# One transfer for the first slice of G, a shorter warm-up, one more pair loaded slice by slice, and a new written-out order, in a weight-gradient matmul

## The chip, the cores and the metric

The kernel runs on one core of a Trainium2 chip. The metric is the time of one launch on the device in microseconds (us); smaller is better. The profile names the engines PE (TensorE matmul), PEld (TensorE weight load), DVE (VectorE), ACT (ScalarE), POOL (GpSimd) and SP (SyncE, which here only issues transfers).

## The reference: what is computed

```python
batch, m, k, n = 16, 512, 1024, 768
grad_weight = np.einsum('bmk,bmn->kn', input, grad_output)   # float32 in, float32 out
```

Batch and m are both summed over, so with X as 8192 x 1024 and G as 8192 x 768 the output is X transposed times G, 1024 x 768.

## The kernel before

**Slices and blocks.** The 8192 rows are cut into 64 slices of 128 rows, two slices to a load entry u = 0 to 31 (`LOADS`). A matmul takes 128 columns of an X slice as weights and half of a G row, 384 columns, as the moving operand. The output has four quadrants: A (upper half of K, left half of N), B (upper, right), C (lower, left), D (lower, right), each of four blocks q = 0 to 3 of 128 rows. A token such as `C2` means block 2 of quadrant C.

**Plain entries and pairs.** Entries of kind "s" (u = 0 to 3 and 31, ten slices) are multiplied directly, 16 matmuls a slice. Entries of kind "P" (u = 4 to 30, 27 pairs) are multiplied in the manner of Strassen and Winograd: seven products of sums instead of eight products, so 28 matmuls a pair and not 32. The products are summed in the blocks 1, 5, 6, 7 and in A, B and C. The operand sums are made by DVE in bfloat16, three for X (`x0.u`, `x1.u`, `x2.u`, lines 199, 201, 203) and three for G (`g0.u` to `g2.u`, lines 209, 211, 213). At the end the blocks are joined: the close of a last block adds the block that it shares (line 360, DVE; lines 355 and 356 for a 5 block), and for some blocks a merge `w` does that addition ahead of time on POOL, from SBUF to SBUF (line 395).

**Loads.** Slices 0 and 1 of X and slice 0 of G come as float32 over the queues of ACT and SP (lines 145 to 148) and are rounded to bfloat16 by DVE and ACT (`round_by`, line 217). All else comes over POOL's queue, which rounds on the way: entry u = 1 one slice at a time (lines 175 and 177), entries from `MERGED` = 2 on as one transfer of G and one of X (lines 170 and 171). All the transfers of POOL stand ahead of its merges in its order.

**Order.** Nothing is scheduled by a compiler on PE, DVE, ACT and POOL: the string `PLAN` is the order of work, token by token, and every engine runs its part of it in that order. `C2@5.1` opens block C2 in PSUM bank 5 and multiplies it by one item (slice or pair); `C2.3` goes on for three items. `cC2` closes a block with ACT where it may and `vC2` with DVE (a copy if the sum in SBUF is new or was carried along, else an addition, lines 363, 365, 367). `fC2@5` copies the running sum back into a bank with ACT (line 295), so that the next close is a copy. `z` and `y` lay a partial sum aside and add it later (lines 379 and 388), `r` is a rounding. A bank can be opened or filled again only when its close has read it. Blocks A0 to A3 share the banks 0 to 2 throughout and are closed at the very end. A last close is followed by the store of its block, on SP, and on ACT for a part of the last (line 342).

**Warm-up.** Until the first data are there PE multiplies constants (`WARMUP`, line 153): one bfloat16 matmul of 512 columns, two float32 ones of 512, one bfloat16 one of 512. A float32 one is two instructions in the trace.

**The roundings at the start.** Before the plan's first token DVE rounds G columns 0 to 191, X columns 0 to 127, 128 to 255 and 512 to 767, and ACT rounds G columns 192 to 383, X columns 256 to 511 and 768 to 1023; the right half of G and all of slice 1 follow as tokens `r0` to `r4`.

Of the kernel before, what the change touches and what calls it, by code (L numbers as in the profile page):

```python
# [9 lines left out]
P = 128  # L10
# [5 lines left out]
    "A0.1 A2.1 C0@7.1 A3.1 C2@6.1 cC0 r0 C3@3.1 C1@4.1 cC2 A1.1 vC3 B1@5.1 cC1 B2@7.1 D3@6.1 r1 D0@3.1 r4 r2 "  # L16
    "D1@4.1 cB1 D1.1 A0.1 B2.1 cD1 D0.1 B0@5.1 cD3 A3.1 vD0 A2.1 r3 A1.1 B3@6.1 vB0 cB2 B3.1 D3@4.1 B0@3.1 "
    "D2@7.1 vD3 D2.2 B0.1 vB3 B1@5.1 cD2 B1.1 A3.1 C3@4.1 vB1 C3.1 C2@6.2 vC3 A2.1 B3@7.1 C1@5.3 B3.1 B0.1 "
    "vC1 A1.2 C2.1 vB3 B1@4.1 D1@5.1 zcC2.20 D1.1 vB1 B2@7.2 A0.1 vB0 A0.1 A2.1 vD1 D3@6.2 D0@4.1 vB2 D0.1 "
    "A3.1 C3@5.1 vD0 D2@3.1 C0@7.2 vD3 C0.2 vD2 C0.1 C3.2 B3@6.2 vC3 B1@3.2 A3.1 vC0 D3@5.2 vB1 A1.2 B2@4.1 "  # L20
    "vD3 B2.1 D2@3.1 A0.1 yC2.20 A0.1 A3.1 D0@7.1 vB2 D0.1 A2.2 vD2 B0@5.2 D1@4.1 vD0 D1.3 vB0 C0@7.2 A3.1 "
    "vD1 A3.1 A1.1 vC0 B3.1 D2@5.3 fC1@7 B3.1 D0@4.1 vD2 D0.1 A0.2 vD0 fD3@5 C1.3 vB3 C1.1 A2.2 g0.4 cC1 "
    "C3@4.1 B2@6.1 fC2@3 B2.1 g1.4 D3.2 fB0@7 vB2 C3.1 C2.1 cD3 C2.1 g2.4 C2.1 x0.4 C2.2 A2.1 12@5.1 cC2 C3.1 "
    "x1.4 A1.2 c12 x2.4 11@6.1 C0@3.1 fC1@5 vC3 B0.3 c11 vC0 A3.1 C1.1 A0.1 B3@6.1 cC1 61@3.1 B1@4.1 vB3 cB0 "
    "B1.2 c61 73@5.1 g0.5 71@6.1 10@7.1 vB1 13@3.1 x0.5 13.1 A1.1 12@4.1 c13 10.1 A3.1 v12 71.1 c10 73.1 "
    "50@3.1 x1.5 c71 50.1 11@4.1 g1.5 51@7.1 c50 51.1 v11 60@6.1 c73 60.1 61@3.1 g0.6 c51 A2.1 53@5.1 v61 "
    "53.1 fC0@4 A0.1 63@7.1 c53 g2.5 63.1 52@3.1 g1.6 52.1 70@5.1 g2.6 70.1 c52 C0.1 x0.6 C0.1 A1.1 A3.1 cC0 "
    "72@3.1 x2.5 72.2 x1.6 70.1 73@4.1 A0.1 c70 x2.6 63.1 60.1 v73 A2.1 c63 B0@5.2 g0.7 c72 B2@4.2 c60 B2.1 "
    "vB0 62@7.1 fC1@3 62.1 g1.7 62.1 B3@6.1 vB2 B3.1 c62 C1.2 g2.7 C2@4.1 fC0@7 vB3 C2.2 f13@5 C1.1 x0.7 A2.1 "
    "A0.1 cC1 C0.1 11@6.1 vC2 11.1 f51@3 A1.1 13.1 v11 13.1 51.2 x1.7 c13 A3.1 53@6.1 cC0 x2.7 53.1 52@4.1 "  # L30
    "c51 52.1 v53 71@5.2 f50@7 C3@3.1 g0.8 C3.1 f12@6 C3.1 50.1 g1.8 50.1 12.1 g2.8 12.2 x0.8 A2.1 C3.1 c12 "
    "A1.1 A3.1 vC3 52.1 71.1 50.1 x1.8 zc52.20 73@6.2 v71 fB1@3 A0.1 61@4.2 x2.8 c50 61.1 72@5.1 v73 72.1 "
    "fB2@7 B1.2 v72 f10@6 B1.2 B2.1 v61 B2.1 cB1 63@5.1 g0.9 63.1 f51@4 10.3 fC2@3 x0.9 10.1 A1.1 cB2 A3.1 "
    "A2.1 g1.9 51.1 zc63.5 x1.9 51.1 62@7.1 c10 g2.9 62.2 x2.9 c51 A0.1 C2.1 v62 fB3@5 C2.1 60@6.2 y63.5 60.1 "
    "fB0@7 B3.2 v60 cC2 B3.1 11@4.2 y52.20 cB3 B0.2 f13@3 g0.10 B0.1 53@6.2 cB0 13.1 x0.10 13.2 f70@7 A3.1 "
    "11.1 g1.10 c13 A1.1 53.1 x1.10 70.1 f52@5 70.1 v11 70.2 A0.1 g2.10 fB2@4 52.1 x2.10 52.1 C1@3.1 c70 v53 "
    "C1.2 c52 B2.1 C3@7.1 vC1 C3.1 f72@5 B2.1 C0@6.1 vC3 C0.1 cB2 C0.1 72.1 g0.11 f73@3 B1@7.2 A2.1 c72 x0.11 "
    "A2.1 A1.1 f71@4 73.2 vC0 73.1 f63@5 71.1 g1.11 71.1 c73 71.1 x1.11 A0.1 72@6.1 c71 g2.11 72.1 63.1 x2.11 "
    "63.1 fB0@4 63.1 v72 61@3.2 c63 61.1 g0.12 B0.1 fC2@6 B0.1 60@5.1 v61 60.1 cB0 A3.1 g1.12 C2.2 v60 12@3.2 "
    "cC2 12.1 x0.12 12.1 fC3@4 B1.1 A1.1 A2.1 f53@5 g2.12 A3.1 vB1 C3.1 f51@6 C3.1 53.1 v12 53.1 cC3 50@7.2 "  # L40
    "x1.12 50.1 fC1@4 50.1 g0.13 A0.1 c53 51.2 x2.12 51.1 C1.1 g1.13 B3@5.1 c51 B3.1 v50 B3.1 f13@3 C1.1 "
    "52@6.1 vB3 52.1 cC1 13.2 x0.13 13.1 f62@4 11@5.2 c13 11.1 x1.13 A0.1 62.1 v52 62.1 f70@3 62.2 g2.13 "
    "61@7.2 c62 x2.13 70.2 v61 fC0@6 70.1 B2@4.2 v11 c70 B2.1 C0.2 vB2 f71@3 C0.1 A3.1 f73@7 10@5.1 g0.14 "
    "10.3 B1@4.1 x0.14 A2.2 zcB1.4 71.2 10.1 x1.14 f51@4 71.1 73.1 g1.14 73.1 c71 x2.14 73.1 51.1 g2.14 51.1 "
    "c73 A1.2 v10 c51 A0.1 B3@7.1 g0.15 cC0 B3.1 A3.1 63@3.1 vB3 fB1@6 63.2 B0@5.1 g1.15 f70@4 B0.1 v63 B0.1 "
    "B1.2 g2.15 72@7.2 cB1 vB0 72.1 70.1 C2@3.1 x0.15 f52@5 C2.3 53@6.2 vC2 53.1 70.1 52.1 v53 52.2 72.1 "
    "x1.15 f11@6 C1@3.2 v72 C1.1 c52 A2.1 A0.1 vC1 c70 13@7.2 60@5.1 yB1.4 f10@3 60.2 g0.16 60.1 11.2 x0.16 "
    "11.1 10.2 c11 13.1 v60 A1.2 f62@4 A3.1 x1.16 A3.1 f71@6 A2.1 v13 50@5.3 g1.16 50.1 f12@7 g0.17 62.2 "
    "zc50.18 62.1 12.1 g1.17 12.1 c62 12.1 g2.16 12.1 x2.16 71.1 fB1@4 71.1 g2.17 C3@5.1 c12 C3.1 x2.15 C3.2 "
    "x0.17 C3.1 10.1 A2.1 C0@7.1 c10 vC3 C0.2 c71 C0.1 x1.17 A3.1 A0.1 fB2@6 x2.17 A0.1 B0@3.1 g0.18 B0.2 "  # L50
    "B2.1 vC0 B2.3 vB0 B1.3 g1.18 C2@7.2 cB1 g2.18 73@5.2 cB2 vC2 73.1 C1@3.1 f61@4 C1.1 x0.18 C1.1 A1.1 "
    "zc73.3 51@6.2 vC1 51.2 C2@5.1 x1.18 fB3@3 61.2 vC2 61.3 x2.18 f53@5 63@7.2 g0.19 63.1 c61 63.1 53.2 v63 "
    "f52@4 53.1 B3.2 g1.19 f12@7 B3.1 v51 B3.1 A0.1 c53 52.1 12.1 cB3 12.1 13@5.1 x0.19 f71@6 13.2 12.1 "
    "72@3.1 x1.19 72.2 v13 72.1 71.2 v12 71.1 70@5.2 g0.20 70.1 f60@7 70.1 52.1 v72 52.2 60.1 g1.20 60.1 c52 "
    "x2.19 60.2 c71 A1.1 v70 A1.1 11@3.1 f10@6 g2.19 11.2 x0.20 11.1 fB3@5 10.3 v11 A3.2 c10 A3.1 x1.20 A2.1 "
    "fB1@3 73@4.1 x2.20 73.2 g0.21 B3.1 60.1 62@6.1 v73 62.1 c60 62.2 g2.20 B1.1 C0@4.1 g1.21 C0.1 cB1 y50.18 "
    "C0.1 C2@7.1 cB3 C2.1 g2.21 B1@3.2 v62 fB2@5 A2.3 x0.21 B2.3 vC0 C2.1 71@6.2 zcC2.1 vB1 A0.1 51@4.1 cB2 "
    "51.1 g0.22 51.1 A0.1 f72@5 50@7.1 v71 50.3 g1.22 50.1 C1@3.2 v50 C1.1 72.2 x1.21 C3@7.2 g2.22 c72 C3.1 "
    "v51 C3.2 C1.1 x0.22 A1.3 zcC1.10 12@6.1 f63@5 12.1 x1.22 12.1 53@4.1 f13@3 53.1 v12 53.2 63.1 x2.21 63.2 "
    "x2.22 63.1 B0@6.1 g0.23 B0.1 c63 B0.2 v53 B0.1 A0.1 vC3 A0.1 f70@4 13.3 f52@5 x0.23 13.1 70.2 c13 70.1 "  # L60
    "g1.23 A3.1 fC0@7 x1.23 A3.1 52.1 vB0 52.3 g2.23 61@3.2 g0.24 61.3 70.1 C0.1 v61 C0.1 c70 C0.1 62@6.1 "
    "y73.3 c52 62.2 cC0 x2.23 B3@4.3 g1.24 f71@5 B3.1 v62 A3.2 A0.1 x0.24 A0.1 A2.3 vB3 71.3 x1.24 73@4.2 "
    "yC1.10 c71 73.2 fB2@7 50@6.1 g2.24 50.1 v73 11@5.3 x2.24 B2.1 f60@4 B2.1 v11 B2.1 f62@3 B2.1 60.1 g0.25 "
    "60.1 cB2 60.2 x0.25 A1.3 72@7.1 x1.25 72.2 g1.25 72.1 A3.1 yC2.1 62.1 zc72.15 62.1 60.1 x2.25 A2.1 "
    "B1@5.1 c60 g2.25 B1.2 c62 B1.2 B0@4.1 f10@3 B0.1 vB1 B0.1 53@7.2 g0.26 53.1 10.2 g1.26 10.2 x0.26 10.2 "
    "51@5.2 c10 x1.26 51.2 y72.15 51.1 f52@3 50.1 A3.1 vB0 zc51.21 50.2 A0.1 x2.26 A0.1 fB2@4 63@5.1 g0.27 "
    "63.3 52.1 g1.27 53.1 v50 B2.2 zc53.18 52.1 v63 52.1 cB2 12@6.2 g2.26 12.2 x0.27 12.1 B3@7.2 g2.27 B3.1 "
    "11@4.1 v12 11.3 y53.18 C0@5.3 vB3 C0.1 C2@6.2 g0.28 fC3@7 C2.3 vC0 C2.1 C3.1 g1.28 C3.2 x1.27 C3.2 vC2 "
    "52.1 61@5.1 cC3 61.1 y51.21 61.1 c52 61.1 A2.1 v11 A2.2 13@6.1 x0.28 13.4 x1.28 72@7.2 zc13.12 72.1 "
    "x2.28 61.1 f73@3 70@4.1 v72 70.2 f71@6 70.1 v61 70.1 73.2 g2.28 73.1 x2.27 73.1 C3@5.1 g0.29 71.4 g1.29 "  # L70
    "A2.1 C1@7.1 c71 g2.29 C1.2 c73 x0.29 C1.4 A3.1 g0.30 A3.1 zcC1.4 A3.1 C3.1 f11@3 v70 A1.4 x1.29 f62@4 "
    "12@7.1 g1.30 12.1 A0.1 y13.12 A0.2 11.1 vC3 11.1 10@6.2 x0.30 10.2 11.1 13@5.1 v10 13.1 c11 12.1 62.1 "
    "x1.30 f61@6 62.2 v12 62.1 f72@3 62.1 61.1 v13 f71@7 61.1 A2.1 v62 72.1 f60@5 72.1 71.1 v61 71.1 f51@4 "
    "60.2 g2.30 60.1 f52@6 60.1 v72 60.1 51.2 v60 f70@3 51.1 wC2 51.1 52.1 v71 52.2 A3.1 f63@7 v51 A3.2 70.1 "
    "fC0@5 70.1 63.2 yC1.4 63.1 wD1 63.1 C0.1 v70 C0.1 fC1@4 C0.2 v63 C0.1 A0.2 vC0 fD1@7 A0.1 C1.2 v52 fC2@5 "
    "C1.1 A2.2 f73@3 A1.3 vC1 fB1@6 wD2 D1.2 x2.30 73.2 cD1 x2.29 B1.2 vA3 B1.1 fB2@7 B1.2 v73 fD2@4 B1.2 "
    "C2.1 vA2 C2.1 f53@3 C2.2 vA1 C2.1 53.2 cC2 53.1 vB1 53.1 B2.1 fC3@5 B2.1 v53 B2.1 fD3@2 B2.3 f50@6 C3.1 "
    "vA0 C3.2 wB3 50.1 vB2 50.3 vC3 D2.1 fB0@7 D2.1 D3.1 v50 D3.1 cD2 B0.2 fD0@5 B0.3 fB3@3+4 vD3 B0.2 D0.2 "
    "vB0 B3.4 vD0 B3.2 cB3 "
# [3 lines left out]
WARMUP = [("b", 512), ("f", 512), ("f", 512), ("b", 512)]  # L83
# [369 lines left out]
```

## Time and profile before

| | |
|---|---|
| time of three runs | 161.98 us median (161.97 to 162.1) |
| the profiled execution | 161.87 us, of which its span is 160.1 us |
| PE busy | 154.8 us, 97% of the span |
| DVE busy | 145.1 us, 91% |
| ACT, POOL busy | 99.3 us (62%), 39.1 us (24%) |
| matmuls on data (line 324) | 996 |
| warm-up matmuls | 6 instructions, 0.78 to 5.15 us |
| POOL's transfers from line 170 / 171 | 30 of 384 KB / 30 of 512 KB, as written to SBUF |
| transfers | busy throughout to about 140 us, 209 to 216 GB/s as written |

The time of the profiled execution is 1.77 us more than its span: what lies before the first and after the last instruction. Times in the views are counted from the span's start. PE's instructions overlap: a 384-column matmul shows 326 ns from start to end, while the next one starts 162 ns after it, so a busy share near 100% says only that PE was not idle for long.

### The profile page before, as it was taken

What the parts mean: (1) busy time and instruction counts of PE and PEld (TensorE: products, weight loads), DVE (VectorE), ACT (ScalarE), POOL (GpSimd) and SP (SyncE); (2) the same over time, 40 slices, a digit from 0 to 9 for tenths busy, and PEclk for the clock granted to TensorE, in tenths of its full rate; (3) what the DMA queues carried; (4) which work ended last, traced back from release to release, by engine and by line L of the source; (5) the groups of instructions that cost most, each with busy time, mean ns of one, the idle gap of its engine ahead of it and who ended that gap; (6) DMA issues with size and microseconds to landing.
All of it is one profiled execution on the core that took longest, in us unless ns stands there. A gap on an engine that the chain in (4) does not pass through costs nothing.

```text
span 160.1 us, 2989 instructions
## 1 busy us (share of the span) xinstructions
PE 154.8 (97%) x1002; PEld 98.9 (62%) x1129; DVE 145.1 (91%) x335; ACT 99.3 (62%) x227; POOL 39.1 (24%) x73
## 2 busy tenths in 40 slices
PE   8999999999999999999999999999999999999891
PEld 3466666567677777776656566666666566666461
DVE  0579899999999999999999999999989999999991
ACT  3741028779699998985785756365465244586760
POOL 7442212222221222222122222212222100024120
PEclk9999999999999999999999999999999999999999
DMA  5999999999999999999999999999999999930696
GB/s 176 296 211 212 214 215 215 212 213 216 209 214 214 212 211 214 214 213 214 213 214 213 213 212 212 214 214 209 214 214 212 214 213 214 213 60 18 184 365 218
DMA packets 12446, 33.41 MB, mean 209 GB/s; under 512 B 1424, under 2 KB 4240, under 8 KB 12432
## 3 DMA queue, kind: packets, MB, share of 16 engines
q0 software_dynamic: 9360, 28.64, 90.4%
q1 hardware_dynamic: 2640, 3.41, 6.6%
q10 hardware_dynamic: 432, 1.18, 2.0%
q8 instruction: 8, 0.13, 0.3%
q14 instruction: 6, 0.05, 0.1%
HBM read 58.72 MB, written 3.15 MB: 386 GB/s over the span
## 4 chain that ended last, share of the span: by engine, by line
PE 78%; DMA 16%; POOL 1%; DVE 1%; issue 1%; DVEq 0%; POOLq 0%
PE bank L324 78%; DMA xp<-in_input_dram 16%; POOL gp L175 1%; DVE xp L203 1%; POOL xp L177 0%; DVE acc L365 0%; DVEq L365 0%; POOLq L437 0%
## 5 line engine op out<-in xcount | busy, mean ns | idle before, releaser
L324 PE MATMUL bank<-gp,xp 128*128 128x384 bf16 (+2 forms) x672 | 108.9, 307 | 1.1 <-DVE xp L203 0.5
L324 PEld LDWEIGHTS <-xp 128*128 128x128 bf16 x672 | 61.7, 97 | 32.4 <-DMA xp<-in_input_dram 2.0
L324 PE MATMUL bank<-ge,xe 128*128 128x384 bf16 x324 | 64.0, 326 | 0.0
L324 PEld LDWEIGHTS <-xe 128*128 128x128 bf16 x324 | 31.2, 97 | 15.3 <-DVE xe L201 0.2
L363 ACT COPY macc<-bank 128x384 f32<-128x384 f32 x63 | 28.8, 482 | 17.5 <-PE bank L324 17.3
L367 DVE TENSOR_TENSOR acc<-bank,acc 128x384 f32<-128x384 f32 x62 | 32.4, 552 | 2.8 <-PE bank L324 2.6
L295 ACT COPY bank<-macc 128x384 f32<-128x384 f32 x60 | 28.2, 485 | 6.2 <-DVE macc L367 2.8
L367 DVE TENSOR_TENSOR macc<-bank,macc 128x384 f32<-128x384 f32 x55 | 29.9, 552 | 1.1 <-PE bank L324 0.6
L295 ACT COPY bank<-acc 128x384 f32<-128x384 f32 (+2 forms) x43 | 20.1, 478 | 14.7 <-DVE acc L367 12.1
L171 POOL DMA_DIRECT2D xp<-in_input_dram x30 | 15.9, 532 | 51.9 <-DMA xp<-in_input_dram 22.8
L170 POOL DMA_DIRECT2D gp<-in_grad_output_dram x30 | 16.0, 532 | 38.3 <-PE bank L324 18.8
L363 ACT COPY acc<-bank 128x384 f32<-128x384 f32 (+1 forms) x42 | 19.4, 479 | 8.2 <-PE bank L324 7.8
L199 DVE TENSOR_TENSOR xe<-xp 128x1024 bf16<-128x1024 bf16 x27 | 18.5, 685 | 0.1
L209 DVE TENSOR_TENSOR ge<-gp 128x768 bf16<-128x768 bf16 x27 | 14.8, 550 | 0.3 <-DMA gp<-in_grad_output_dram 0.3
L203 DVE TENSOR_TENSOR xp<-xp,xe 128x512 bf16<-128x512 bf16 x27 | 11.7, 440 | 0.2
L201 DVE TENSOR_TENSOR xe<-xe,xp 128x512 bf16<-128x512 bf16 x27 | 11.3, 419 | 0.3
L379 ACT COPY aside<-bank 128x384 f32<-128x384 f32 x13 | 6.2, 479 | 8.0 <-PE bank L324 7.8
L323 PEld LDWEIGHTS <-xp 128*128 128x128 bf16 x81 | 7.9, 98 | 4.8 <-DMA xp<-in_input_dram 0.4
L395 POOL TENSOR_TENSOR acc<-acc,macc 128x384 f32<-128x384 f32 x4 | 4.2, 1061 | 22.8 <-DVE macc L360 16.5
L211 DVE TENSOR_TENSOR ge<-gp,ge 128x384 bf16<-128x384 bf16 x27 | 9.5, 352 | 0.2
L213 DVE TENSOR_TENSOR gp<-ge,gp 128x384 bf16<-128x384 bf16 x27 | 9.5, 351 | 0.1
L360 DVE TENSOR_TENSOR acc<-bank,macc 128x384 f32<-128x384 f32 (+2 forms) x14 | 6.3, 489 | 0.1
(23 smaller groups left out, 37.6 us busy)
## 6 DMA issues: line engine op xcount, KB each, us to landing
xp<-in_input_dram POOLq DMA_DIRECT2D x30, 512.0 KB, 16.9
gp<-in_grad_output_dram POOLq DMA_DIRECT2D x30, 384.0 KB, 16.7
out_dram<-acc SPq DMA_DIRECT2D x12, 192.0 KB, 2.1
xf<-in_input_dram ACTq DMA_DIRECT2D x2, 512.0 KB, 4.9
gp<-in_grad_output_dram POOLq DMA_DIRECT2D x3, 192.0 KB, 6.5
out_dram<-acc SPq DMA_DIRECT2D x6, 96.0 KB, 2.2
xp<-in_input_dram POOLq DMA_DIRECT2D x2, 256.0 KB, 7.8
gf<-in_grad_output_dram SPq DMA_DIRECT2D x2, 192.0 KB, 4.4
```

The source lines that it names most:

```text
L170: nc.gpsimd.dma_start(out=gp, in_=G[rows, :].rearrange("(p m) n -> p m n", m=2))
L171: nc.gpsimd.dma_start(out=xp, in_=X[rows, :].rearrange("(p m) k -> p m k", m=2))
L199: nc.vector.tensor_sub(out=xe[:, 0:2, :], in0=x[:, 1::-1, :], in1=x[:, 3::-2, :])
L201: nc.vector.tensor_sub(out=xe[:, 2, :], in0=xe[:, 0, :], in1=x[:, 0, :])
L203: nc.vector.tensor_add(out=x[:, 1, :], in0=x[:, 2, :], in1=xe[:, 2, :])
L209: nc.vector.tensor_add(out=ge[:, 0:2, :], in0=g[:, 0:2, :], in1=g[:, 1::2, :])
L211: nc.vector.tensor_add(out=ge[:, 2, :], in0=g[:, 3, :], in1=ge[:, 0, :])
L213: nc.vector.tensor_add(out=g[:, 1, :], in0=ge[:, 2, :], in1=g[:, 2, :])
L295: nc.scalar.copy(out=tile_[:, t0 : t0 + c1 - c0], in_=sum_of(p, q)[:, c0:c1])
L324: nc.tensor.matmul(tile_[:, t0 : t0 + c1 - c0], stat, mov[:, c0:c1], start=start, stop=True, skip_group_check=True,)
L363: nc.scalar.copy(out=d, in_=b)
L367: nc.vector.tensor_add(out=d, in0=b, in1=d)
```

## The change

Four things change at the head, and the whole order is new.

- Slice 0 of G comes as one transfer of whole rows on SP's queue, in place of a left and a right half.
- The third warm-up matmul has 384 columns in place of 512.
- `MERGED` is 3 in place of 2: entry u = 2 (slices 4 and 5) comes as four transfers, G and X of slice 4, then G and X of slice 5.
- The seven roundings that stood ahead of the plan become tokens `r10` to `r16`, so the plan sets their order.
- `PLAN` is another order of the same products. It has six merges on POOL in place of four, 12 sums laid aside in place of 13, 246 closes in place of 251 and 104 fills in place of 102. `LOADS`, the banks, the number of matmuls and their widths are the same.

```diff
-WARMUP = [("b", 512), ("f", 512), ("f", 512), ("b", 512)]
+WARMUP = [("b", 512), ("f", 512), ("f", 384), ("b", 512)]
-MERGED = 2
+MERGED = 3
-    nc.sync.dma_start(out=gf[:, LEFT], in_=G[0:P, LEFT])
+    nc.sync.dma_start(out=gf, in_=G[0:P, :])
     nc.scalar.dma_start(out=xf[0], in_=X[0:P, :])
-    nc.sync.dma_start(out=gf[:, RIGHT], in_=G[0:P, RIGHT])
     nc.scalar.dma_start(out=xf[1], in_=X[P : 2 * P, :])
...
-    round_by("DVE", g0, gf, 0, 192)
-    round_by("ACT", g0, gf, 192, NH)
-    round_by("DVE", x0, xf[0], 0, P)
-    round_by("ACT", x0, xf[0], 2 * P, 4 * P)
-    round_by("DVE", x0, xf[0], P, 2 * P)
-    round_by("DVE", x0, xf[0], 4 * P, 6 * P)
-    round_by("ACT", x0, xf[0], 6 * P, 8 * P)
-    ROUNDINGS = [
+    ROUNDINGS = {
+        0: ("DVE", g0, gf, NH, N),
+        1: ("DVE", x1, xf[1], 4 * P, 6 * P),
+        2: ("DVE", x1, xf[1], 0, 2 * P),
+        3: ("ACT", x1, xf[1], 6 * P, 8 * P),
+        4: ("ACT", x1, xf[1], 2 * P, 4 * P),
+        10: ("DVE", g0, gf, 0, 192),
+        11: ("ACT", g0, gf, 192, NH),
+        12: ("DVE", x0, xf[0], 0, P),
+        13: ("ACT", x0, xf[0], 2 * P, 4 * P),
+        14: ("DVE", x0, xf[0], P, 2 * P),
+        15: ("DVE", x0, xf[0], 4 * P, 6 * P),
+        16: ("ACT", x0, xf[0], 6 * P, 8 * P),
+    }
```

The places of the order that the text below speaks of, of before and of after:

```diff
 PLAN = (
-    "A0.1 A2.1 C0@7.1 A3.1 C2@6.1 cC0 r0 C3@3.1 C1@4.1 cC2 A1.1 vC3 B1@5.1 cC1 B2@7.1 D3@6.1 r1 D0@3.1 r4 r2 "
...
-    "C1.1 A2.2 f73@3 A1.3 vC1 fB1@6 wD2 D1.2 x2.30 73.2 cD1 x2.29 B1.2 vA3 B1.1 fB2@7 B1.2 v73 fD2@4 B1.2 "
-    "C2.1 vA2 C2.1 f53@3 C2.2 vA1 C2.1 53.2 cC2 53.1 vB1 53.1 B2.1 fC3@5 B2.1 v53 B2.1 fD3@2 B2.3 f50@6 C3.1 "
-    "vA0 C3.2 wB3 50.1 vB2 50.3 vC3 D2.1 fB0@7 D2.1 D3.1 v50 D3.1 cD2 B0.2 fD0@5 B0.3 fB3@3+4 vD3 B0.2 D0.2 "
-    "vB0 B3.4 vD0 B3.2 cB3 "
+    "r0 r16 r10 r11 r15 D3@7.1 r13 r12 r14 C2@5.1 vD3 D0@6.1 C0@4.1 cC2 A3.1 B0@3.1 vC0 B3@7.1 A1.1 cB0 A2.1 "
...
+    "11@7.1 B3@6.1 51@3.1 g0.5 10@4.1 vB3 10.1 x0.5 11.1 13@6.1 c10 A1.1 g1.5 A2.1 c11 51.1 v13 53@4.1 71.1 "
...
+    "f12@5 71@7.2 g0.8 50.1 fC3@6 50.1 12.2 g1.8 C3.2 g2.8 C3.1 x0.8 C3.1 A0.1 A3.1 cC3 A1.1 x2.7 12.1 52.1 "
...
+    "A3.2 g2.15 f12@4 C2@7.1 x0.15 C2.1 cB3 C2.1 C1.2 cB1 y71.9 C1.1 70@6.2 cC1 x1.15 12.2 vC2 f60@3 12.1 "
...
+    "g0.29 71.2 C1@4.1 x1.28 C1.1 c71 C1.2 zcC0.15 C1.2 f62@5 61@3.1 yC0.15 61.3 y51.7 61.1 10.2 vC1 10.1 "
+    "A1.2 x0.29 A3.1 f70@4 A3.2 f11@7 v61 A0.1 A2.3 x2.27 70.1 y73.4 70.3 x1.29 70.1 A0.1 g0.30 12@3.1 c70 "
+    "12.2 62.1 f71@4 g1.30 62.2 x2.28 62.1 11.1 g1.29 11.1 c62 11.2 x0.30 11.1 10.1 12.1 c11 13@5.2 v12 c10 "
+    "13.2 f61@7 A3.1 x1.30 A2.1 A1.1 g2.30 A1.1 f72@6 v13 61.1 f62@3 61.1 72.1 g2.29 72.1 f60@5 72.1 v61 62.2 "
+    "A0.1 x2.29 f51@7 60.2 v62 60.3 x2.30 fC1@3 51.2 v60 51.1 A0.2 v72 71.2 C1.1 f63@6 C1.1 wC2 v71 C1.2 "
+    "f70@5 A3.1 A1.1 vC1 A1.1 A2.1 fC2@4 A2.1 v51 63.3 70.1 C2.2 v70 f73@7 wB1 C2.3 v63 f52@5 A3.1 73.2 vA2 "
+    "fC3@3 wC0 73.2 fB2@6 52.1 vA0 52.2 cC2 C3.1 wD1 C3.1 v52 C3.1 fC0@4 C3.1 B2.3 vA1 B2.1 f53@5 B2.1 wD2 "
+    "B2.1 C0.1 v73 f50@1 C0.3 vC3 53.1 fD2@7 53.2 vC0 53.1 fB1@3 50.2 vB2 50.1 fD1@0 50.1 D2.1 v53 fD3@4 D2.1 "
+    "D1.2 cD2 D3.2 B1.1 vA3 fD0@7 B1.1 wB3 B1.1 fB0@5 B1.1 vD3 B1.2 cD1 v50 B1.1 B0.2 cB1 B0.3 fB3@3+4 B0.2 "
+    "D0.2 vB0 B3.4 vD0 B3.2 cB3 "
 ).split()
```

## The prediction

> **What bounds the kernel now.** I read the page first: PE, then the transfers.
>
> ```profile
> span 160.1 us, 2989 instructions
> PE 154.8 (97%) x1002; PEld 98.9 (62%) x1129; DVE 145.1 (91%) x335; ACT 99.3 (62%) x227; POOL 39.1 (24%) x73
> DMA  5999999999999999999999999999999999930696
> ```
>
> PE is hardly ever idle, and the transfers are busy for 35 of 40 slices. The matmuls' own work is a constant: 996 of them, 351,744 columns in all, at 2.4 columns a ns and 2.5 ns more each (384 columns start 162.5 ns apart wherever no wait lies between) make 149.05 us, and the last ends 0.16 us after its columns. The first starts at 5.04 and PE ends at 156.72, so 156.72 - 5.04 - 149.05 - 0.16 = 2.46 us are waits. Only these can go. Then the chain of work that ended last, in order of time, to see where they lie:
>
> ```profile
> 3.50 8.41 DMA xp<-in_input_dram
> ...
> 12.20 17.80 DMA xp<-in_input_dram
> ...
> 30.05 117.88 PE bank L324 x776
> 147.93 1.24 DVE xp L203 x2
> 149.17 0.05 issue
> 149.22 7.51 PE bank L324 x51
> ```
>
> Up to 30.0 the arrival of X sets the pace, then PE alone, but for one wait at 148. PE's waits over the whole run:
>
> ```profile
> PE bank L324 <- DVE xp L203: 0.5, 1, 0.5
> PE bank L324 <- DMA xp<-in_input_dram: 0.4, 2, 0.3
> PE bank L324 <- DVE gp L217: 0.2, 1, 0.2
> ```
>
> Measured from start to start, which counts the drained pipeline too, they cost 0.62 (at 149.2), 0.34 and 0.42 (at 16.2 and 30.0) and 0.41 us (at 6.8). The other 0.67 is some fifteen waits of at most 0.12 us, mostly for a bank. The timeline shows what the wait at 148 is:
>
> ```profile
> 147.54 1.00 POOL L395 TENSOR_TENSOR acc<-acc,macc 128x384 f32<-128x384 f32 x1 [1.54 <-DVE macc L356]
> 147.84 1.31 DVE L203 TENSOR_TENSOR xp<-xp,xe 128x512 bf16<-128x512 bf16 x2
> ```
>
> Two sums x2 run beside a merge on POOL. By the instructions of line 203 in that stretch they took 979 and 412 ns; the first ended 0.28 us after the merge, and every other one takes about 0.42. `B1.2` waits for the second. The Trainium skill (SBUF — State Buffer, Who interferes with whom) says that a DVE instruction with two SBUF inputs and a GpSimd instruction that reads SBUF exclude each other, whichever is second waiting for the first; the 979 ns agree.
>
> **The chip's transfers set floors.** A load that lands at t lets the matmuls that lie behind its first use end no earlier than t + 0.05 + their work + 0.16. The two orders can be compared by this count alone. X of pair 29 lands at 134.11 (issued at 116.70, 17.4 to landing). In the order before, its first use is matmul 848 (`A2.1`), behind which 21.49 us of work lie: floor 155.82. After, it is matmul 845 (`10.1`), with 152 matmuls and 51,456 columns still to do, 21.44 + 0.38 = 21.82 us: floor 134.11 + 0.05 + 21.82 + 0.16 = 156.14. The next ones of after are pair 30 (138.42, 17.42 us: 156.06) and pair 15 (73.44, 82.33: 155.99); of before, pair 17 (155.90). So the new order leans harder on the transfers, yet its floor lies 0.58 under where before ended, 156.72.
>
> **Part by part.**
>
> *G of slice 0 in one transfer.* The halves land at 4.40 and 6.35, X of slice 0 at 4.73. Both queues move packets in turn, so X now shares with all of G: 917 KB must pass before it lands in place of some 760, at 394 GB/s (the stretch 2.6 to 5.0) 0.4 us more. I take 5.1 for X and 4.9 for G; ends are 4.73 and 5.9 (X of slice 1 now takes 5.9 from issue) and, for G, 4.40 and 6.35. The order begins with `D3`, which waits for `r16`: 5.1 + 0.02 + 0.41 (ACT, 256 columns of X) + 0.05 = 5.58 for the first matmul, 0.54 later than 5.04. `C2` waits for `r11` behind `r16` on ACT, 0.09 more. The 0.41 at 6.8 goes, since the right half is there (`r0`, 0.36, lies ahead of X's landing). SP's queue has one issue less (0.42) with nothing behind it until the stores. The seven moved roundings are the same instructions, on engines that wait for the landing anyway.
>
> *Warm-up.* Two instructions, 0.853 apart for 512 columns, lose a quarter: 2 x 0.21 = 0.43, so PE is free at 4.6 in place of 5.0. The first matmul waits for data until 5.58: worth nothing, if the clock is granted as before (a rival below).
>
> *Slices 4 and 5 one by one.* POOL issues four in place of two, 2 x 0.53 = 1.06 us more; its next issue waits until 7.79 for a landing, 2.15 idle, so they are hidden. Entry 1, which comes so already, takes 4.41 us from G of slice 1 to X of slice 3, the merged ones 4.28 to 4.35: +0.1 for all later landings, against some 0.1 won by the larger first packets. I take +0.05, ends -0.1 and +0.15. X of slice 4 lands near 14.1, not 16.19, so the 0.34 at 16.2 goes.
>
> *The order to 30 us.* Pair 5 is first used by matmul 165 (`10.1`), as before. Without a wait it would come at 5.58 + 0.09 + 23.77 = 29.44; X lands at 30.00. So 0.60 of wait, and the head's 0.54 changes only its length. The head's parts come to zero; up to about 0.5 us more delay would be absorbed as well.
>
> *30 to 134 us.* Floors instead of small waits: pair 8 adds 0.25, pair 15 0.23, pair 29 0.16 and the 0.05 of the shift. DVE keeps its load (70 instructions in 30 to 60 us either way), and PE is held back enough for the closes to keep up.
>
> *The tail.* `x0.30` starts when X of pair 30 lands, at 138.4; from it to `x2.30` DVE has nine instructions of 0.27 to 0.60, 3.7 in all, so the sums are done by about 142.7. The first merge, `wC2`, waits for `v72`, which lies behind `x2.30` in DVE's own order; no sum and no `y` follows it. So the 0.62 cannot come back in this form. Six merges in place of four, 1.00 each (one 1.25): what is queued behind one matters on ACT. `52.2` ends with 8.1 us of matmuls to go, at 148.1; `v52` is two DVE instructions, 0.47 and 0.55, so `wD2` starts at 149.2 and ends at 150.2, and `fD2`, `fB1` and `fD1` follow on ACT at 0.42 each. `fD1` ends at 151.6; `D1.2` comes 4.4 before PE's end, at 151.8. Hidden by 0.2. The last closes (`vB0`, `vD0`, `cB3`) and their stores stand as before.
>
> *Sum.* Waits and start: 0.54 + 0.09 + 0.60 + 0.25 + 0.23 + 0.16 = 1.87 against 2.46, that is -0.59, and +0.05 for the landings; small waits behind 134 us apart from the wait at 149 were 0.1 before and I count half of that, +0.05: -0.49. PE ends at 156.2. The profiled execution took 161.87, 0.11 under the median of 161.98; from the one the sum is 161.38, from the other 161.49: 161.4. A change of 0.2%, 0.32 us, is about what can be told from none here.
>
> **Rivals.**
>
> *The clock falls behind (slower).* The warm-up's bf16 matmul of 512 columns takes 0.58 us, while later ones take 0.326 for 384 and 0.272 for 256, which would be 0.38 for 512; the last warm-up matmul, at 4.57, still takes 0.58. So PE runs at about half speed until 5.0, 4.2 us after its start. Now it falls idle at 4.6 for a microsecond. If it had to be busy that long once more, 5.6 to 9.8 at half speed would lose 2.1 us; partly, 1.0. The 0.5 of slack goes first: PE ends 0.5 to 1.6 later than forecast, 161.9 to 163.0. It is slower by over 0.2% from a loss of 1.4 on. Against it: an interval of 4 us is 75% busy still, and the wait of 0.4 at 6.8 before did no harm. The Trainium skill (TensorE: Matmul & The Clock Gate, What's actually happening) gives a free-running window of 3.4 us that must have been busy; by that the next grant would come near 8.4 and the loss be 1.4, an estimate that ends at 162.3. No row shows what share of a window counts as busy. Chance 0.13.
>
> *Transfers come later, or the tail stalls (no change to tell).* Landings later by 0.3, as pair 15's is (4.61 us behind pair 14's, where 4.31 is usual), or merges of 1.25: then `fD1` ends at 151.9, a little past `D1.2`, and PE at 156.4 to 156.5. 161.6 to 161.8; 0.22. For it: the floor is the transfers', so each delay there counts in full.
>
> *Faster still.* Pair 29 lands 0.4 late by its usual pace (4.71, not 4.31). Without this and with earlier landings the end is 155.7: 160.9. Chance 0.07.
>
> *The forecast*, 161.1 to 161.65: 0.52. Some other stall that I can't place, of either size: 0.06, taken as slower. Faster by over 0.2%: 0.52 + 0.07 = 0.59; within: 0.22; slower: 0.13 + 0.06 = 0.19. Range 160.9 to 162.4: the upper end reaches into the clock's case, and what lies above or below is under 0.2.
>
> **What would show it.** Right: first matmul at 5.4 to 5.7, no wait at 6.8 and 16.2, one of 0.5 to 0.7 for X at 30, small ones at 43, 73 and 134, sums of line 203 all near 0.42, PE's end at 156.0 to 156.4. Wrong: matmuls of over 0.5 us behind 5.6 (the clock), X of pair 5 landing away from 30.0, or PE waiting for ACT's fills between 150 and 153.

## The result, and the profile after

The changed kernel takes 163.11 us (median of seven runs, 162.35 to 163.39) against 161.97 (161.79 to 162.2): a ratio of 1.006, interval 1.0045 to 1.0074. It is slower, and the forecast of 161.4 us, with a range up to 162.4, was wrong. The seven runs of the changed kernel lie in two groups, 162.35 and 162.45, and 163.10 to 163.39; the kernel before has one. The profiled run, at 162.45, is of the lower group, so its trace can show only the first part of the loss, and the larger part had to be looked for in other executions. Line numbers of this kernel are one lower than before (323 is the matmul on data, 216 a rounding, 202 the sum x2).

The head of the page of the changed kernel:

```profile
span 160.6 us, 2991 instructions
PE 153.5 (96%) x1002; PEld 99.6 (62%) x1129; DVE 140.8 (88%) x327; ACT 101.2 (63%) x230; POOL 41.8 (26%) x77
DMA  5999999999999999999999999999999999922596
```

PE is 1.3 us less busy than before while the span is 0.5 us longer: PE has lost time to waits. Its chain of work that ended last (start, length, what) says where:

```profile
10.07 12.04 DMA xp<-in_input_dram
22.12 0.05 issue
22.16 8.82 PE bank L323 x59
30.98 0.54 DVE acc L366
...
44.25 0.04 issue
44.29 112.96 PE bank L323 x748
```

Before, the transfers set the pace up to 30.0, at entry 5's X, and PE alone after it. Now PE waits at 22.16 for X of entry 3, which lands at 22.12 and had landed at 20.54 before. Entry 5's X (30.13) is not waited for at all. In its place a stretch of closes and sums on DVE, from 30.98 to 44.25, carries the chain, and only then PE runs alone. PE's waits over the run (in total, times, longest):

```profile
PE bank L323 <- ACT xp L216: 1.7, 1, 1.7
PE bank L323 <- DMA xp<-in_input_dram: 0.9, 1, 0.9
...
PE bank L323 <- DVE acc L366: 0.3, 1, 0.3
```

The first is the idle time between the warm-up (its last matmul ends at 4.17) and the first matmul on data at 5.92. The second is X of entry 3. From start to start the waits cost 1.02 at 22.2, then 0.444 at 31.6, 0.117 at 32.2 and 0.225 at 44.3, all three behind DVE. PE ends at 157.24 (before: 156.72).

Why X of entry 3 comes late is in the transfers of 20.0 to 21.2 us (queue, kind: packets, MB, share of 16 engines in this stretch):

```profile
q0 software_dynamic: 88, 0.22, 96.0%
q8 instruction: 1, 0.02, 5.1%
```

A single packet of 16 KB on the queue that the page calls "instruction" holds one of the 16 DMA engines for 0.97 us, from 20.1 on. X of entry 3 is in transfer just then, and lands some 1.4 us later than the 20.75 that the forecast had for it. The kernel before has the same packet at 21.36, behind the landing of entry 3's X; there it fell on G of entry 4, which nothing needed yet.

So far the trace. Two theories came out of it, and the expectations below go by them. **Theory 1, the code load:** the order needs entry 3's X at the moment it lands, the packet falls on it, and a wait of about 1 us comes before the slack at entry 5 that was to absorb delays. This is the lower group's loss. **Theory 2, the clock:** with PE idle from about 4.5 to 5.8 the full clock is not granted in some executions until several us of data matmuls have run at half speed. This is the upper group. The rivals were a general delay of the transfers, and the new order's own waits on DVE.

### The profile page after: what moved, and what is told of

It is laid out like the page before. It is cut to its first block, busy times and chain, and to the rows that moved or that the text cites. A ratio compares the mean times of both kernels' runs of the same rounds, so it can differ in the third digit from the quotient of the medians.

```text
span 160.6 us, 2991 instructions
## 1 busy us (share of the span) xinstructions
PE 153.5 (96%) x1002; PEld 99.6 (62%) x1129; DVE 140.8 (88%) x327; ACT 101.2 (63%) x230; POOL 41.8 (26%) x77
## 4 chain that ended last, share of the span: by engine, by line
PE 76%; DMA 12%; DVE 8%; issue 1%; POOL 1%; DVEq 0%; POOLq 0%
PE bank L323 76%; DMA xp<-in_input_dram 12%; DVE acc L366 2%; DVE macc L366 2%; DVE xe L198 1%; DVE ge L208 1%; DVE ge L210 1%; POOL gp L174 1%; DVE gp L212 1%; DVE xe L200 1%; DVE xp L202 0%; DVE acc L364 0%; DVEq L364 0%; POOLq L436 0%
## 5 line engine op out<-in xcount | busy, mean ns | idle before, releaser
L323 PEld LDWEIGHTS <-xp 128*128 128x128 bf16 x672 | 62.9, 97 | 33.4 <-ACT xp L216 2.3
L323 PE MATMUL bank<-ge,xe 128*128 128x384 bf16 x324 | 64.8, 326 | 0.0
L323 PEld LDWEIGHTS <-xe 128*128 128x128 bf16 x324 | 31.3, 97 | 14.5 <-DVE xe L198 0.4
L366 DVE TENSOR_TENSOR macc<-bank,macc 128x384 f32<-128x384 f32 x61 | 32.7, 550 | 1.6 <-PE bank L323 1.1
L294 ACT COPY bank<-macc 128x384 f32<-128x384 f32 x57 | 27.1, 486 | 8.9 <-DVE macc L366 3.4
L362 ACT COPY acc<-bank 128x384 f32<-128x384 f32 (+1 forms) x46 | 21.4, 475 | 15.5 <-PE bank L323 14.9
L366 DVE TENSOR_TENSOR acc<-bank,acc 128x384 f32<-128x384 f32 x49 | 26.1, 551 | 5.1 <-PE bank L323 5.0
L294 ACT COPY bank<-acc 128x384 f32<-128x384 f32 (+2 forms) x48 | 22.3, 477 | 12.0 <-DVE acc L366 9.4
L169 POOL DMA_DIRECT2D gp<-in_grad_output_dram x29 | 15.3, 528 | 34.9 <-PE bank L323 21.1
L394 POOL TENSOR_TENSOR acc<-acc,macc 128x384 f32<-128x384 f32 x6 | 5.9, 1001 | 22.0 <-DVE macc L359 18.5
L322 PEld LDWEIGHTS <-xp 128*128 128x128 bf16 x79 | 7.7, 98 | 4.8
L322 PEld LDWEIGHTS <-xe 128*128 128x128 bf16 x48 | 4.7, 98 | 2.6 <-DVE xe L198 0.2
```

What stands on the lines that cost most here:

```text
L169: nc.gpsimd.dma_start(out=gp, in_=G[rows, :].rearrange("(p m) n -> p m n", m=2))
L294: nc.scalar.copy(out=tile_[:, t0 : t0 + c1 - c0], in_=sum_of(p, q)[:, c0:c1])
L322: nc.tensor.ldweights(stat)
L323: nc.tensor.matmul(tile_[:, t0 : t0 + c1 - c0], stat, mov[:, c0:c1], start=start, stop=True, skip_group_check=True,)
L362: nc.scalar.copy(out=d, in_=b)
L366: nc.vector.tensor_add(out=d, in0=b, in1=d)
```

## Experiments

**The change once more.** No edit.

> The changed kernel once more, for a second trace. Seven runs of it lie in two groups, 162.35 to 162.45 and 163.10 to 163.39; the profiled one is of the first. Theory 1 (transfers: a load of PE's code at 20.1 us delays X of entry 3 to 22.1, and PE waits 1.0 for it): every run has this wait, the groups differ by where the landings fall, and a run of the second group shows X of entry 3 or later landings some 0.7 us later still. Theory 2 (clock: PE is idle from 4.2 to 5.9 now, and in most runs the full clock is granted only after the first data): a run of the second group shows 384-column matmuls 320 ns apart somewhere behind 5.9, for at least 1.4 us, since half of that is lost. A run of the first group shows neither.

162.35 us (162.17 to 163.02, seven runs), ratio 1.0035 (1.0019 to 1.005), again in two groups: four at 162.17 to 162.35, three at 162.87 to 163.02. The profiled run, 162.18, belongs to the lower: the packet at 19.8, X of entry 3 at 21.81, a wait of 0.88 at 21.9, and then 0.445, 0.114 and 0.226 on DVE; PE ends at 156.95. The groups and the wait are the kernel's own.

**The old warm-up.**

```diff
-WARMUP = [("b", 512), ("f", 512), ("f", 384), ("b", 512)]
+WARMUP = [("b", 512), ("f", 512), ("f", 512), ("b", 512)]
```

> The changed kernel with the old warm-up (third matmul of 512 columns), nothing else. Theory 2: PE is busy 0.2 to 0.4 us longer before the idle stretch, so the second group gets rarer or goes: median 162.4 to 162.7. Theory 1: no change, median 163.1.

162.44 us (162.14 to 162.5, eleven runs), ratio 1.0025 (1.0016 to 1.0033). Nothing at 162.87 or above is left: the upper group is gone, the lower stays, with a wait of 0.94 for X of entry 3. The two losses are separate. The runs still stand around two values, four at 162.14 to 162.22 and seven at 162.42 to 162.50; the trace is of the first kind, and the difference stays open (last section).

**A warm-up that reaches into the data's time.**

```diff
-WARMUP = [("b", 512), ("f", 512), ("f", 384), ("b", 512)]
+WARMUP = [("b", 512), ("f", 512), ("f", 512), ("f", 512), ("b", 128)]
```

> The changed kernel with three float32 warm-up matmuls of 512 columns and a short bfloat16 one, so that PE is busy until about 5 to 6 us and the idle stretch ahead of the data goes. Theory 2: no second group at all, median 162.2 to 162.5. Theory 1: median 163.1, or 0.2 more where the warm-up runs past the first data.

162.07 us (161.97 to 162.53, eleven runs), ratio 1.0015 (1.0006 to 1.0024). Data matmuls begin at 6.645, 0.9 later than in the second trace of the change (5.753), and yet PE ends at 156.87, 0.08 earlier. The packet, which comes as PE gets on, is now at 20.72, behind the landing of entry 3's X at 20.61, and PE does not wait for it. In this trace a head that is 0.9 us later costs nothing, since it moves the packet off the load that matters. The waits of 0.445, 0.115 and 0.223 on DVE are there unchanged. Four of the eleven runs stand at 162.40 to 162.53, and no trace shows what they lose.

**Weight loads added early, to move the packet.** Every second matmul from 12 to 61 gets a weight load of no use ahead of it, 25 in all.

```diff
-SPARE_LOADS = range(200, 455)
+SPARE_LOADS = [*range(12, 62), *range(200, 455)]
```

> The changed kernel with 25 more weight loads on PE (every second matmul from the 13th to the 61st loads its weights twice), which move the place in PE's instructions at which the next 16 KB of code are fetched by some 12 matmuls, 2 us: from 20.1 to about 18.1. Theory 1: X of entry 3 lands about 0.6 earlier (21.5), PE's wait at 22.2 shrinks from 1.0 to about 0.4, and the time falls by 0.3 to 0.6 in either group. Theory 2: the time stays within 0.2, since the extra loads lie beside matmuls.

162.76 us (161.77 to 163.09, twelve runs), ratio 1.0032 (1.0013 to 1.0051). The packet comes at 17.9, 1.9 us sooner than in the second trace of the change. So it follows the number of PE's instructions: 25 more at about two for each 0.16 us are 2.0 us. In the eleven traces of the new order and its variants the packet starts after 208 to 215 matmuls and weight loads, here after 208. The queue's row for 17.5 to 19.2 us here, then the row of PE's wait for X in the change's second trace and here:

```profile
q8 instruction: 1, 0.02, 3.6%
PE bank L323 <- DMA xp<-in_input_dram: 0.7, 1, 0.7
PE bank L323 <- DMA xp<-in_input_dram: 0.3, 1, 0.3
```

X of entry 3 lands at 21.45, the wait from start to start is 0.42 instead of 0.88, and the lower group moves from 162.17 to 162.35 down to 161.77 to 162.06, by about 0.3 to 0.4. The upper group (seven of twelve, 162.75 to 163.09) hardly moves, which was not expected: it does not lose its time at entry 3.

**A shorter warm-up.**

```diff
-WARMUP = [("b", 512), ("f", 512), ("f", 384), ("b", 512)]
+WARMUP = [("b", 512), ("f", 512)]
```

> The changed kernel with a warm-up of one bfloat16 and one float32 matmul of 512 columns, so that PE is idle from about 2.9 us to the first data at 5.8. Theory 2 (clock): the full clock is granted only after some 3 us of data matmuls; 384-column matmuls start about 320 ns apart from 5.8 to between 9 and 10, 1.6 to 2 us are lost, the wait for X of entry 3 takes 1.0 of it back, and every run lies at 162.9 to 163.5, one group. Theory 1 (transfers alone): the data still start at 5.8 and the time is as before this edit, 162.2 to 162.4.

163.38 us (162.93 to 163.68, four runs), ratio 1.0085 (1.0068 to 1.0101), none of them at 162.2. Data begin at 5.784, and until 10.79, where the trace's record of the granted clock first says full, the 384-column matmuls start 320 ns apart and not 160. Some 2.4 us are lost there, and X of entry 3, at 20.56, is not waited for.

**The change with G of slice 0 in two halves.**

```diff
-    nc.sync.dma_start(out=gf, in_=G[0:P, :])
+    nc.sync.dma_start(out=gf[:, LEFT], in_=G[0:P, LEFT])
+    nc.sync.dma_start(out=gf[:, RIGHT], in_=G[0:P, RIGHT])
```

> The changed kernel with G of slice 0 in two halves again, order and all else as changed. The order begins with D3, which needs the right half, so the first data matmul moves from 5.8 to about 6.8. Theory 1: the wait for X of entry 3 absorbs up to 1.0 of it: median within 0.2 of the changed kernel in its faster group (162.2), and that wait is near zero. If the head counts in full: 163.2. Theory 2: PE is idle a microsecond longer, so the slower group gets more frequent.

164.07 us (161.87 to 165.16, twelve runs). The ratio of 1.008 (1.0048 to 1.0112) is of the seven runs up to 164.09; with the other five, 164.81 to 165.16, which no trace shows, the medians give 1.013. The new order needs the right half early, so data begin only at 6.869 in the profiled run (163.96). Here the record of the clock speaks directly: full at 3.717, half again at 7.130, full at 10.543, steps of 3.413 us. PE was busy for 25% of the first of these stretches. The row of the granted clock, in 40 slices of 4 us:

```profile
PEclk9869999999999999999999999999999999999999
```

Two of the twelve runs, 161.87 and 161.96, are faster than any of the change's, though the head is 1.1 us later. That the clock did not fall in these two fits, but no trace shows it.

**The old kernel with the shorter warm-up, nothing else.**

```diff
-WARMUP = [("b", 512), ("f", 512), ("f", 512), ("b", 512)]
+WARMUP = [("b", 512), ("f", 512), ("f", 384), ("b", 512)]
```

> The kernel before with only the shorter warm-up (third matmul of 384 columns). The data come at 5.04, so PE is idle 0.4 to 0.5 us at most. Theory 2: no harm, 161.9, one group, since it is the idle stretch and not the length of the warm-up that counts; if a window that is a little less busy already costs the grant, a second group some 0.5 higher appears (162.4), what the waits at 16 and 30 us don't take back. Theory 1: 161.9.

161.94 us (161.83 to 162.17, eleven runs) against 161.95: ratio 1.0, 0.9992 to 1.0009. With data at 5.0 the idle stretch is 0.26 us, and the warm-up edit is worth nothing either way. It does harm only together with the later data.

**The change profiled again, to see the upper group.** No edit.

> The change unaltered, profiled once more, to see the slower of its two groups of times (about 162.9) in a trace, if this execution falls in it. Clock theory: an execution near 162.9 shows the granted clock at full only after data matmuls have begun (a window of 3.4 us after the first one, so at about 8 us instead of 3.4 to 4.9), with 384-column matmuls some 320 ns apart until then instead of 160, and PE ends 0.6 to 0.8 later than 156.95; an execution near 162.2 shows the full clock before the first data matmul. Rival, that the slower group comes from a transfer: the clock is full before the data as in the faster group, and a wait longer than 1.0 stands at entry 3 or one appears at entries 5 to 8.

163.22 us, the upper group, and theory 2's picture. PE in two equal stretches from the first matmul on data (window, its length, each engine's busy us and count, ...), here in this run:

```profile
5.77:9.90 4.13, 4.13 (x16) 2.15 (x17) 1.93 (x7) 2.48 (x7) 1.14 (x2) 1.00 1.14 220
9.90:14.03 4.13, 4.13 (x29) 2.62 (x28) 2.44 (x5) 1.50 (x4) 2.11 (x4) 1.00 1.13 207
```

and the first of these stretches in the second trace of the change, in the lower group:

```profile
5.75:9.88 4.13, 4.13 (x29) 2.67 (x30) 2.45 (x8) 3.19 (x9) 1.06 (x2) 1.00 1.14 223
```

The first number in brackets is PE's: 16 matmuls in 4.13 us instead of 29, as busy as ever. (The clock column reads 1.00 before the first record, so spacing is what to look at.) The record first says full at 9.877, and by then 2.0 us are lost from start to start. No X is waited for; the packet comes at 21.64, behind X of entry 3 (20.57). The waits on DVE, 0.444, 0.117 and 0.226, stay. PE ends at 157.99, 1.04 later than in the lower group: 2.0 are lost, the 0.88 at 22 is not. So PE reaches entry 3 after its X has landed, which would be why the upper group did not care where the packet fell.

**Slice 6 before slice 7.** The old warm-up, entry 3 slice by slice too, and the visits around matmul 105 turned round, so that slice 7 is needed 6 matmuls later.

```diff
-MERGED = 3
+MERGED = 4
-... A0.2 vB0 A0.2 A1.1 vC2 A1.1 B3.1 vD2 B3.2 C1.2 cB3 ...
+... A0.2 vB0 A0.1 A1.1 vC2 B3.2 vD2 C1.1 A0.1 A1.1 B3.1 C1.1 cB3 ...
```

> e2_warm (old warm-up of 512) with entry 3 loaded slice by slice too, and the visits at matmul 105 turned round: everything of slice 6 that the open banks take (A0, A1, B3, C1, and the last of B3 on slice 5) goes ahead of the first matmul on slice 7. X of slice 6 should land near 18.5 and X of slice 7 between 20.6 and 21.8, and slice 7 is needed 6 matmuls, 0.96 us, later than now. Theory 1 (the code load on entry 3's X is what the faster group lost): the wait of 0.9 at 22 is gone or under 0.1, a wait of 0.2 to 0.6 for entry 5's X comes back at 30, the waits of 0.44, 0.12 and 0.22 after it stay or shrink, PE ends 156.2 to 156.5, median 161.5 to 161.8. Rival (the waits on VectorE between 31 and 44 set the end whatever comes before them, as when the long warm-up put the first matmul 0.9 later and PE still ended at 156.87): PE ends 156.8 to 157.0, median 162.0 to 162.3.

161.76 us (161.57 to 162.13, eleven runs) against 161.97: ratio 0.9989, 0.9981 to 0.9998, and 0.68 below the kernel that it was made from. X of slice 6 lands at 18.46, X of slice 7 at 21.90, hit by the packet at 19.89 as before, and the wait at 22 is 0.14. The chain of this kernel has no DVE between 30 and 44:

```profile
14.33 11.57 DMA xp<-in_input_dram
25.90 0.28 issue
26.18 17.16 DMA xp<-in_input_dram
43.34 0.09 issue
43.42 112.97 PE bank L323 x748
```

The transfers pace PE up to 43.4, with 0.549 for entry 5's X and 0.381 for entry 8's, as the forecast had it (0.60 and 0.25). PE ends at 156.38. Theory 1 holds; the rival, that the waits on DVE set the end whatever comes first, falls: they are absorbed by the waits for the transfers.

**Slices 4 and 5 as a pair again.**

```diff
-MERGED = 3
+MERGED = 2
```

> The change with slices 4 and 5 as one pair of transfers again, as before (merged from entry 2 on), all else of the change kept: X of slice 4 then lands with slice 5's at about 16.2 instead of 14.0, and the new order needs it at matmul 61, which PE reaches at about 13.9. Theory (loading them one by one is what the new order stands on): a wait of 2.0 to 2.4 at 14, the code load moves behind entry 3's X with it and the wait of 0.9 at 22 goes, the waits on VectorE after 30 take back up to 0.8; PE ends 157.4 to 158.3, median 162.6 to 163.5 in its faster group. Rival (loading one by one costs as much in queue time as it brings): PE ends within 0.2 of 156.95, median 162.2 to 162.4.

162.89 us (162.83 to 162.95, four runs), ratio 1.0057 (1.0042 to 1.0073). The longest of PE's waits on data in this kernel:

```profile
PE bank L323 <- DMA xp<-in_input_dram: 1.4, 1, 1.4
```

It stands at 16.3, 1.53 from start to start (2.0 to 2.4 expected; PE was there 0.8 later than I had reckoned), the wait at 22 is gone, and PE ends at 157.70. The new order stands on slice 4 coming early. Loading one by one is no loss.

**The old kernel without the merge that delays x2.**

```diff
-C1.1 A2.2 f73@3 A1.3 vC1 fB1@6 wD2 D1.2 ...
+C1.1 A2.2 f73@3 A1.3 vC1 fB1@6 D1.2 ...
-... vC3 D2.1 fB0@7 D2.1 D3.1 v50 D3.1 cD2 ...
+... vC3 D2.1 fB0@7 D2.1 D3.1 v50 D3.1 vD2 ...
```

> The kernel before without the merge wD2 on POOL: D2 is closed by DVE with an addition in place of ACT with a copy (one DVE instruction of 0.47 more, near the end). The sums x2.30 and x2.29 and their place stay. If the merge is what holds x2.30 up: the sums of line 203 at 148 take 0.42 each, B1.2 does not wait, PE ends 0.6 earlier, 161.3 to 161.4, a kernel faster than both. If something else holds it up (DVE late, an operand late): the wait at 149.2 stays near 0.6 and the time at 161.9.

161.81 us (161.65 to 161.91, eleven runs), ratio 0.9988 (0.9979 to 0.9996). The two sums, in the timeline of this kernel (start, length, engine, line):

```profile
147.94 0.75 DVE L203 TENSOR_TENSOR xp<-xp,xe 128x512 bf16<-128x512 bf16 x2
```

They take 0.410 and 0.415 us without the merge on POOL, where they took 979 and 412 ns, and the wait of 0.618 is 0.05. PE ends at 156.25, 0.47 sooner, yet the last store lands at 159.12, 0.06 sooner: it is issued 0.35 sooner and takes 2.30 us to land instead of 2.02. Ahead of the last two, stores follow one another on SP about 0.5 us apart and land 0.52 to 0.55 apart. So most of the gain ends among the stores; that it is their queue that holds them is not shown.

**Slice 6 first, with a warm-up up to the data.** The kernel of two sections above, with

```diff
-WARMUP = [("b", 512), ("f", 512), ("f", 512), ("b", 512)]
+WARMUP = [("b", 512), ("f", 512), ("f", 512), ("b", 512), ("b", 512), ("b", 384)]
```

> e10_sixfirst with two more bfloat16 matmuls in the warm-up (512 and 384 columns, some 0.37 together at full clock and 0.75 at half), so that PE is idle for less than 0.4 us before the data instead of 0.7. Theory 2 (what the clock grants depends on how much of the last window of 3.41 us PE was busy, and the idle stretch before the data is what it misses): no window that ends before 6.9 has less than 80% of PE's time, so the full clock comes with data at 6.6 at the latest; a head that is 0.2 to 0.4 late is taken up by the wait for entry 5's X (0.55 in e10); no execution above 162.0, where e10 had three of eleven, median 161.55 to 161.75. Rival (the upper three of e10 come from elsewhere, the transfers or the chip's state): they stay, median 161.7 to 161.9.

161.71 us (161.56 to 161.85, eleven runs) against 161.94: ratio 0.9985, 0.9976 to 0.9994. The three runs of 162.0 to 162.13 that the warm-up before it had are gone, though three of eleven against none can be chance, and 161.71 lies in the range of either theory. In the profiled run the record says full at 6.432, so this run began its data (6.005) at half speed and lost some 0.2 there. PE ends at 156.49. Its median is the lowest here, 0.15% ahead of the kernel before and not to be told from that of slice 6 first; a faster kernel than before is to be had from this change, but by less than 0.25%.

## Why the prediction was wrong

**The first step that failed: "worth nothing, if the clock is granted as before".** The warm-up was costed at nothing, with the clock as a rival at 0.13. The mechanism was named, and so was the size (2.1 us lost at half speed; 2.0 measured). The chance was wrong: 9 of the 15 executions of the unaltered change that were timed are in the upper group. That "an interval of 4 us is 75% busy still" and that "the wait of 0.4 at 6.8 before did no harm" were the reasons against it, and neither was one: the wait of 0.4 lay inside a window that was otherwise full. Counted back from the records in steps of 3.413 us, windows in which PE was busy for 78% and 86% ended with the full clock (the change's first trace, the halves), and those of 66%, 67%, 69% and 71% did not (old kernel without the merge; short warm-up; long warm-up; upper-group trace). Keeping the clock took less: it stayed full after windows of 49%, 64% and 67% (the change's first trace, the pairs, the spare loads) and fell only after the one of 25% (the halves). The upper group's two windows before the grant, to 3.05 and to 6.46, had 67% and 71%: in the first PE had started at 0.78, in the second it sat idle from 4.78 to 5.77. Where the windows lie differs from trace to trace (the first grants lie at 3.43 and 4.90 in the two of the lower group), hence, as I read it, the two groups. The Trainium skill (TensorE: Matmul & The Clock Gate, What's actually happening) gives this free-running window as 3413 ns; the records agree. By its rule of one busy window the prediction's estimate was 162.3; the profiled run shows 163.22.

The rest of that error is the slack. The rival let 0.5 go into the wait for entry 5's X. But the order has 0.79 of waits on DVE behind that point (0.444, 0.117, 0.226), which I had taken as covered: "PE is held back enough for the closes to keep up". That is true where the transfers hold PE back, as in the kernel with slice 6 first, and false where PE comes late for another reason.

**The second: "I take +0.05, ends -0.1 and +0.15" for all later landings.** That put X of entry 3 at 20.75 at the latest, and the pace was right (20.53 to 20.61 in the eight traces where the packet comes after it, the one of before among them), but 21.45 to 22.12 was measured where the packet falls on it. I compared floors for the pairs alone, and none for entry 3. The new order reaches it with no slack at all. The trace of before had the packet, at 21.36, and the 2.94 us that G of entry 4 took behind X of entry 3 (1.86 is usual); I did not ask what it would fall on if it came sooner, as it does in the new order, by 1.2 us and more. PE is not further on by then (99 matmuls on data have started at 20.11, before 100); in the three traces of the old order the packet starts after 227 to 229 matmuls and weight loads, in the new order after 208 to 215, and what makes this difference is not shown. The Trainium skill (Runtime: NRT & Kernel Launch, Instruction fetch mechanics) says that an engine's instructions are refilled in 16 KiB blocks of 256, mostly hidden. The size agrees, and so does the shift of 1.9 us by 25 added loads; that it was hidden holds for the engine and not for the load that shares its DMA engine.

**Where it was right.** The waits at 6.8 and 16.2 went. The first matmul came at 5.75 to 5.92 against 5.58, since X landed at 5.27 to 5.44 and not 5.1. The tail is as reckoned: the sums of line 202 took 411 to 418 ns, the first `wC2` follows them, and `fD3` cost 0.08. From 44 us on PE needs 112.96 to 112.97 us for its 748 matmuls in the traces of the change, of its upper group, of the long warm-up and of slice 6 first, whatever came before, so pairs 15 and 29 (0.23 and 0.16 in the sum) bind nothing, and the sum was too careful there.

**What the forecast was a forecast of.** With both losses taken away, as with slice 6 first, PE ends at 156.38 against my 156.2, and the time is 161.76 against 161.4. That PE's end comes so near is in part luck: a start 0.19 later than reckoned and the wait of 0.14 at 22 stand against the 0.39 of pairs 15 and 29 that was never waited. The rest of the difference is behind PE: there the span ends at 159.95, 3.56 us after PE, before at 160.10, 3.39 after it. The closes and stores did stand "as before": the last store lands 2.43 us after PE's end, against 2.47. The 0.2 lies between that landing and the end of the span, 1.13 us against 0.92, where POOL starts the program's closing instructions 0.2 after SP has done its own, instead of 0.03 before; why stays open. In the old kernel without the merge the span ends 3.79 after PE, and there it is the stores, the last of which lands 2.88 after PE.

## What to carry to other kernels

Before an order is allowed to lean on a transfer, look at what it has for neighbours: a load that lands within a us of its use can be hit by a 16 KB instruction packet, whose time, within one order, moves with the number of instructions that PE has run. A gap between warm-up and data is not free because PE has nothing to do in it: what counts is PE's busy share of each 3.4 us up to the data, at any position of the window, until the full clock is granted; 71% was not enough to gain it here, and 49% was enough to keep it. And slack is not a sum to spend once: what is behind the wait that absorbs a delay has to be read too.

## What was not expected of the hardware

- Eight packets of 16 KB on the instruction queue run through each trace, 15 to 21 us apart, each 0.89 to 1.4 us on one DMA engine. The first moved X of entry 3 by 0.9 to 1.6 us. In the five traces where it starts within a us of the usual landing, the load under way lands 2.0 to 2.1 us after the packet's start, though the packet itself takes 0.89 to 0.98; what the second us is stays open.
- The clock fell back from full to half after one window at 25% busy, and came back 3.413 us later.
- A head that is 0.9 us later left PE's end no later (156.87 against 156.95), since the packet then missed the load that PE was waiting for.
- What stays open: what share of a window between 71% and 78% is enough, and the smaller split (162.2 and 162.45) of the change with the old warm-up. Two ways to it are on record. The change's first trace, at 162.45, shows X of slice 0 landing 0.17 us later, and the packet starting 0.3 us later, than the second, at 162.18. And where the clock's windows lie as in the upper-group trace, the old warm-up, which at half speed ends at 5.20 (old kernel without the merge), would fill 83% of the window to 6.46; the full clock would come there, and some 0.35 us be lost, an estimate from these traces.
